# Sample attention of a hybrid decoder step as one list of steps over all its segments

## The chip, the cores and the metric

One NeuronCore of a Trainium2 chip runs the whole program in one launch. The metric is the device time of that launch in microseconds (us), as the median of several runs. Engines: PE is TensorE, ACT ScalarE, DVE VectorE, POOL GpSimd, SP SyncE (it only issues DMAs).

## What is computed

Two layers of a decoder, each with a convolution group and a sparse-attention group side by side. There are 512 prompt tokens and 8 sample tokens, one for each of 8 sequences that have 4096 past positions in a paged cache. For each sample token and each of 4 key heads the reference does:

```
s_c = q . k_cmp * scale            # 64 compressed blocks, softmax -> p_c, o_c
imp = sum of p_c over the 4 query heads of a key head
top 16 of 64 blocks by imp (first and last blocks forced)
s_s = q_rot . k_sel * scale        # 16 chosen blocks x 64 positions, softmax -> o_s
s_w = q_rot . k_win * scale        # last 512 positions, softmax -> o_w
o   = g0 * o_c + g1 * o_s + g2 * o_w
```

The chosen blocks differ by sequence and by head, so their keys and values (64 floats each) are fetched from the cache in HBM by indirect DMA. Beside this, in the same stage, the 520 tokens are multiplied by the columns of `w_in` that feed the convolution (values, gates), the attention gate `za` and the convolution gate `zc`; a 31-tap convolution, a layer norm and two gates follow.

## The kernel before

A tile framework orders each engine's instructions: program order gives the priority, and an instruction is placed once a simulated timeline holds it ready, so a lower-priority one can go ahead. `issue_after(mark)` forbids instructions of a block to be placed ahead of `mark` on the mark's engine. Each layer has four stages: `phase_a1` (first projections, and the compression of the cache), `phase_a2` (lines 815 to 1262, the stage of this change), `phase_b` (prompt attention) and `phase_c` (output product and next norm).

**The matrix product.** `gemm` (L322) works through jobs of 256 columns; a yield closes each chunk of four 128-row slices of weights (24 matmuls per half chunk, two halves), and one more closes the job. A 512 KB weight DMA (L332) fills `wf`; for each half, `split` (L373) makes a rounded part `wh` on ACT (L374) and the rest `wl` on DVE (L375), three buffers of each, at high priority; PE then runs three products (L350 to L352). `g.pe_mark` is the last matmul of the chunk (L357).

**The stage `phase_a2`.** `_interleave` (L136) mixes two generators, `proj2` with weight 80 and `sample` with weight RATE_S = 90: whichever has the fewer steps per weight goes next. `proj2` (L921) has 75 yields in the first layer and 80 in the second. `_behind` (L148) wraps `sample`: what it emits in a step is placed on PE behind the latest `g.pe_mark`. Ahead of both, L832 to L836 load the convolution weights, transpose them on PE (`pw`, L835) and copy them on DVE (`cwt`, L836).

**The generator `sample`** (L932). Its first step scores the compressed blocks, ranks them and makes the gather indices `six` (L1023). Then, for each half `rho` of the sequences, `comp_seg` and three calls of `segment` follow one another: the first half of the chosen blocks, the window, the second half. A segment covers four sequences. `keys_of` (L1068) fetches a tile of 128 positions with four indirect DMAs on POOL, one for each head (L1112, into `G2`, two buffers), copies keys (`kc`, L1122) and values (`vt`, L1131) on ACT, and transposes the keys on PE (`kpt`, L1126); a page of the newest positions comes with one more (L1097). All of a tile's work is emitted in one step:

```
for h in range(4):
    nc.gpsimd.indirect_dma_start(out=G[:np_, h, :], ...)
nc.scalar.activation(kc_..., G[:np_, :, 0:64], AF.Copy)
for hp in range(2):
    nc.tensor.transpose(pts[hp][:, j * 128:j * 128 + np_], kc_[...], ident[...])
nc.scalar.activation(vt_..., G[:np_, :, 256:320], AF.Copy)
if j < 3:
    yield None
```

There are three tiles per sequence in the first half and four in the second: 56 tiles and 224 gathers a layer besides the eight page rows. After a segment's last sequence, `segment` (L1148) runs its scores (`pss`, L1163), the maximum (`st_m`, L1176), the exponential (`ssc`, L1179), the transposes (`ptp_s`, L1190), the copy (`pts`, L1195 or L1198) and the products with the values (`pos_`, L1203) in one step; the sums into the output (`o_a`, `o_s`, L1038 and L1040) are a step of their own. The next segment's keys are emitted behind that. PSUM gives this generator three buffers (`mi`): two hold `kpt`, one `pss`. At the end L1249 transposes `o_s` (`pto`), and `phase_b` begins.

Of the kernel before, what the change touches and what calls it, by code (L numbers as in the profile page):

```python
# [10 lines left out]
F32 = mybir.dt.float32  # L11
# [18 lines left out]
SV = 5  # L30
# [3 lines left out]
RATE_S = 90  # L34
G2B = 2
# [286 lines left out]
def gemm(g, jobs, rhs, evac):  # L322
    nc, tc = g.nc, g.tc
    gps, wp = (g.gp, g.sp.gp2), g.wp
    for wsrc, c0, mi_, hs, (k0, k1), width in jobs:
# [3 lines left out]
        for kc in range(k0, k1, kf):  # L329
# [5 lines left out]
            for k2 in range(0, kf, kh):  # L335
# [479 lines left out]
def phase_a2(g, l, u):  # L815
# [5 lines left out]
    with ExitStack() as s2:  # L821
# [11 lines left out]
        pw = mi.tile([128, 512], F32, tag="mi", name="pw")  # L833
        for i in range(CT):
            nc.tensor.transpose(pw[:, i * CW:(i + 1) * CW], cwn[:, i * 128:(i + 1) * 128], ident[:CW, :CW])  # L835
        nc.vector.tensor_copy(cwt.rearrange("p a b -> p (a b)"), pw[:, :CT * CW])  # L836
# [8 lines left out]
        gst = {}  # L845

# [86 lines left out]
        def sample():  # L933
# [134 lines left out]
            def keys_of(rho, kind, half):  # L1068
                sps = (2 * rho, 2 * rho + 1)
                for s2 in range(2):  # L1070
                    for sp in sps:
                        s = 2 * sp + s2
                        kk = []
                        pts = [mi.tile([128, 512], F32, tag="mi", name="kpt") for _ in range(2)]
                        vt_ = pool.tile([128, 4, 256], F32, tag="sv", name="vt_", bufs=SV)
                        if kind == 1:
                            for part_ in range(2):
                                wt = vt_ if part_ else pool.tile([128, 4, 256], F32, tag="wk", name="wk")
                                nc.sync.dma_start(
                                    wt, a["cache_win"][l, s, :, part_].rearrange("(p j) h d -> p j (h d)", j=4)  # L1080
                                )
                                nc.sync.dma_start(
                                    wt[0:1, 0], kvs_d[s:s + 1, (4 + part_) * 256:(5 + part_) * 256]
                                )
                                if part_ == 0:
                                    for hp in range(2):
                                        for j in range(4):
                                            nc.tensor.transpose(
                                                pts[hp][:, j * 128:(j + 1) * 128],
                                                wt[:, j, hp * 128:(hp + 1) * 128],  # L1090
                                                ident,
                                            )
                        else:
                            for j in range(4):
                                if half == 0 and j == 0:
                                    G = pool.tile([128, 512], F32, tag="G0", name="G0", bufs=1)
                                    nc.gpsimd.indirect_dma_start(  # L1097
                                        out=G,
                                        out_offset=None,
                                        in_=g.rows,  # L1100
                                        in_offset=bass.IndirectOffsetOnAxis(ap=g.fix[:, s:s + 1], axis=0),
                                        element_offset=lrow * ROWF + 512,
                                    )
                                    for hp in range(2):
                                        nc.tensor.transpose(pts[hp][:, :128], G[:, hp * 128:(hp + 1) * 128], ident)
                                    nc.scalar.activation(vt_[:, 0], G[:, 256:512], AF.Copy)
                                    continue
                                jt = 4 * half + j - 1
                                np_ = 64 if jt == 6 else 128
                                G = pool.tile([128, 4, 320], F32, tag="G2", name="G2", bufs=G2B)  # L1110
                                for h in range(4):
                                    nc.gpsimd.indirect_dma_start(  # L1112
                                        out=G[:np_, h, :],
                                        out_offset=None,
                                        in_=g.pages64,
                                        in_offset=bass.IndirectOffsetOnAxis(
                                            ap=six[:np_, s * 4 + h, jt:jt + 1], axis=0
                                        ),
                                        element_offset=lrow * ROWF + 512 + h * 64,
                                    )  # L1120
                                kc_ = pool.tile([128, 256], F32, tag="kc", name="kc_", bufs=1)
                                nc.scalar.activation(  # L1122
                                    kc_[:np_].rearrange("p (h d) -> p h d", h=4), G[:np_, :, 0:64], AF.Copy
                                )
                                for hp in range(2):
                                    nc.tensor.transpose(  # L1126
                                        pts[hp][:, j * 128:j * 128 + np_],
                                        kc_[:np_, hp * 128:(hp + 1) * 128],
                                        ident[:np_, :np_],
                                    )  # L1130
                                nc.scalar.activation(  # L1131
                                    vt_[:np_, j].rearrange("p (h d) -> p h d", h=4), G[:np_, :, 256:320], AF.Copy
                                )
                                if j < 3:
                                    yield None
# [103 lines left out]
            for rho in range(2):  # L1239
                comp_seg(rho)  # L1240
                yield from segment(rho, 0, 0)
                while g.all_kv < l:
                    yield
# [428 lines left out]
```

## Time and profile before

| what | value |
|---|---|
| median of 3 runs | 3020.23 us (3012.37 to 3028.97) |
| profiled execution: time | 3029.22 us |
| profiled execution: span of its instructions | 3027.1 us |
| mean granted TensorE clock | 0.963 |
| PE, DVE, POOL, ACT busy | 90%, 75%, 57%, 48% of the span |
| HBM traffic | 182 GB/s over the span |

The profiled execution is one run of the program; its time is 2.1 us more than the span from its first to its last instruction. Times of rows count from the span's start. A busy PE includes stretches in which its clock was granted at half speed. The stage `phase_a2` runs from about 636 to 1131 us in the first layer and from about 2107 to 2619 us in the second; work of neighbouring stages overlaps its ends.

### The profile page before, as it was taken

Reading aid. Unit: us, or ns where it says so; the run is one execution under the profiler, and the core shown is the slowest. Engines: PE = TensorE matmul, PEld = TensorE weight load, DVE = VectorE, ACT = ScalarE, POOL = GpSimd, SP = SyncE. Lnnn points to the kernel's source line nnn. Section 1 sums busy time; section 2 is a strip of 40 time slices with the busy share of each in tenths; the row PEclk is TensorE's granted clock in tenths of the full one; section 3 lists DMA queues with packets and bytes.
Section 4 is the critical chain, followed back from the end, with each engine's and each line's share of the span. In section 5 each row is a group of like instructions: output and inputs, shape, how many; then the busy total and the mean of one; then the engine's idle time right before and its main releaser. Section 6 shows DMA issues by size and latency. Waiting matters only on the chain. (4 is left out here: it accounts for less than half of the span.)

```text
span 3027.1 us, 53793 instructions
## 1 busy us (share of the span) xinstructions
PE 2716.8 (90%) x18984; PEld 2378.5 (79%) x18984; DVE 2278.1 (75%) x4432; ACT 1446.6 (48%) x3180; POOL 1713.4 (57%) x1610
## 2 busy tenths in 40 slices
PE   7998989988989989888988899999998899998896
PEld 6787878777778778767877788887877778886795
DVE  7899988867877535885889978886687774379756
ACT  5444444433333545773556534444333345468644
POOL 4766676637466456764655735664556565467402
PEclk9999999999989999999999999999999999999998
DMA  8777777645455446316777766775555464563254
GB/s 264 228 210 213 210 210 236 194 119 186 151 160 174 132 148 199 118 36 188 213 237 217 236 208 202 208 228 144 161 181 151 128 214 146 153 186 97 61 161 155
DMA packets 430317, 534.48 MB, mean 177 GB/s; under 512 B 68450, under 2 KB 357362, under 8 KB 429760
## 3 DMA queue, kind: packets, MB, share of 16 engines
q1 hardware_dynamic: 367328, 324.42, 35.9%
q0 software_dynamic: 62720, 206.63, 22.2%
q8 instruction: 149, 2.44, 0.3%
q14 instruction: 120, 0.98, 0.1%
HBM read 484.80 MB, written 64.75 MB: 182 GB/s over the span
## 5 line engine op out<-in xcount | busy, mean ns | idle before, releaser
L350 PE MATMUL g<-uh,wh 128*128 128x256 f32 (+1 forms) x3328 | 962.5, 292 | 18.6 <-ACT wh L374 8.6
L351 PE MATMUL g<-ul,wh 128*128 128x256 f32 (+1 forms) x3328 | 958.9, 290 | 0.0
L352 PE MATMUL g<-uh,wl 128*128 128x256 f32 (+1 forms) x3328 | 944.2, 291 | 9.9 <-DVE wl L375 9.8
L539 POOL DMA_INDIRECT G<-in_cache_kv_pages_dram,gix x512 | 542.5, 1059 | 326.5 <-DVE T L550 161.0
L1112 POOL DMA_INDIRECT G<-in_cache_kv_pages_dram,six x448 | 494.8, 1104 | 336.7 <-issue 115.7
L375 DVE TENSOR_TENSOR wl<-wf,wh 128x512 fp32r<-128x512 f32 x565 | 427.7, 760 | 342.2 <-ACT wh L374 331.5
L350 PEld LDWEIGHTS g<-uh,wh 128*128 128x128 f32 x3328 | 643.9, 194 | 52.5 <-issue 13.9
L351 PEld LDWEIGHTS g<-ul,wh 128*128 128x128 f32 x3328 | 645.0, 194 | 23.2 <-issue 15.3
L352 PEld LDWEIGHTS g<-uh,wl 128*128 128x128 f32 x3328 | 635.3, 194 | 32.2 <-DVE wl L375 12.9
L374 ACT ACTIVATE wh<-wf 128x512 fp32r<-128x512 f32 x616 | 381.7, 625 | 417.4 <-PE g L351 275.2
L375 DVE TENSOR_TENSOR tl<-T,th 128x512 fp32r<-128x512 f32 x512 | 435.5, 869 | 90.4 <-ACT th L374 88.1
L374 ACT ACTIVATE th<-T 128x512 fp32r<-128x512 f32 x512 | 309.8, 624 | 315.9 <-DVE T L550 220.5
L550 DVE STREAM_TRANSPOSE T<-G 128x512 f32<-128x512 f32 x512 | 349.8, 695 | 24.9 <-DMA G<-in_cache_kv_pages_dram,gix 23.2
L887 DVE SCALAR_TENSOR_TENSOR c<-ap,cwt,c 128x512 f32<-128x512 f32 x480 | 339.9, 748 | 0.1
L579 PE MATMUL ca<-tl,w1h 128*128 128x512 f32 x512 | 217.9, 426 | 43.4 <-DVE tl L375 42.9
L375 POOL TENSOR_TENSOR w1l<-w1f,w1h 128x512 fp32r<-128x512 f32 x128 | 170.3, 1332 | 135.2 <-ACT w1h L374 99.4
L578 PE MATMUL ca<-th,w1h 128*128 128x512 f32 x512 | 215.8, 422 | 28.3 <-ACT th L374 17.6
L580 PE MATMUL ca<-th,w1l 128*128 128x512 f32 x512 | 209.5, 409 | 0.2 <-POOL w1l L375 0.2
L1376 POOL TENSOR_TENSOR smx<-smx,su 128x256 f32<-128x256 f32 (+2 forms) x192 | 153.8, 828 | 89.6 <-DVE su L1370 61.2
L1368 ACT ACTIVATE smx<-smx,nm 128x128 f32<-128x128 f32 (+3 forms) x256 | 140.8, 552 | 45.5 <-DVE nm L1364 43.0
L350 PE MATMUL g<-mha,wh 128*128 128x256 f32 (+1 forms) x512 | 146.7, 296 | 12.7 <-ACT wh L374 6.3
L374 ACT ACTIVATE w1h<-w1f 128x512 fp32r<-128x512 f32 x128 | 79.3, 623 | 158.8 <-DMA w1f<-in_cmp_w_dram 98.7
(1179 smaller groups left out, 5236.0 us busy)
## 6 DMA issues: line engine op xcount, KB each, us to landing
wf<-in_w_in_dram SPq DMA_DIRECT2D x220, 512.0 KB
wf<-in_w_out_dram SPq DMA_DIRECT2D x88, 512.0 KB
w1f<-in_cmp_w_dram SPq DMA_DIRECT2D x512, 64.0 KB
out_dram<-in_cache_win_dram SPq DMA_DIRECT2D x16, 1022.0 KB
G<-in_cache_kv_pages_dram,gix POOLq DMA_INDIRECT x512, 5.0
wk<-in_cache_win_dram SPq DMA_DIRECT2D x16, 512.0 KB
qq<-qr_d SPq DMA_DIRECT2D x64, 128.0 KB
G<-in_cache_kv_pages_dram,six POOLq DMA_INDIRECT x448, 3.2
```

The lines of the kernel that those rows point to most:

```text
L350: nc.tensor.matmul(ps[m][h], lh, xh[:, sl], start=first, stop=False)
L351: nc.tensor.matmul(ps[m][h], lh, xl[:, sl], start=False, stop=False)
L352: pe = nc.tensor.matmul(ps[m][h], ll, xh[:, sl], start=False, stop=last)
L374: g.nc.scalar.activation(dst_h, src, AF.Copy)
L375: return (eng or g.nc.vector).tensor_tensor(dst_l, src, dst_h.bitcast(F32), op=ALU.subtract)
L539: nc.gpsimd.indirect_dma_start(out=G[:, i, :], out_offset=None, in_=g.pages, in_offset=bass.IndirectOffsetOnAxis(ap=g.gix[:, un * 4 + hs:u ...
L550: nc.vector.transpose(T.rearrange("p a b c -> p a (b c)"), G[:, :, c * 256:(c + 1) * 256])
L578: nc.tensor.matmul(acc[c], w1h[:, c, e], hi, start=f, stop=False)
L579: nc.tensor.matmul(acc[c], w1h[:, c, e], lo, start=False, stop=False)
L580: nc.tensor.matmul(acc[c], w1l[:, c, e], hi, start=False, stop=la)
L887: ce.scalar_tensor_tensor(c[:, :SEQ], ap[:, j:j + SEQ], cwt[:, i, j:j + 1], c[:, :SEQ], op0=ALU.mult, op1=ALU.add)
L1112: nc.gpsimd.indirect_dma_start(out=G[:np_, h, :], out_offset=None, in_=g.pages64, in_offset=bass.IndirectOffsetOnAxis(ap=six[:np_, s * 4 + ...
```

## The change

`sample` becomes one list of steps over all six segments. Each step first does one pending softmax stage, if there is one, then issues the loads of its own tile, and then finishes (copies, transposes) the tile whose loads the step before issued. The scores, the transposes with the copy, and the value products of a segment are three entries of the pending list, so they fall into the steps that follow, beside the next segment's tiles; both `comp_seg` calls come first. What the sample emits on ACT is placed behind the latest `wh` split as well. The transposes of the convolution weights move behind the first job of `proj2`. RATE_S goes from 90 to 86. The number of buffers, DMAs, matmuls and copies stays as it was. The diff, cut to its core:

```diff
-RATE_S = 90
+RATE_S = 86
 def _behind(g, gen, on=True):
-    g.pe_mark = None
+    g.pe_mark = g.act_mark = None
...
-            for mark in (g.pe_mark if on else None, g.dve_mark):
+            for mark in (g.pe_mark if on else None, g.act_mark if on else None, g.dve_mark):
 # gemm
                     split(g, wh, wl, wf[:, k2:k2 + kh], weights_engine(g))
+                g.act_mark = g.last_act
 # split
-    g.nc.scalar.activation(dst_h, src, AF.Copy)
+    g.last_act = g.nc.scalar.activation(dst_h, src, AF.Copy).ins
 # phase_a2
-        pw = mi.tile([128, 512], F32, tag="mi", name="pw")
-        for i in range(CT):
-            nc.tensor.transpose(pw[...], cwn[...], ident[:CW, :CW])
-        nc.vector.tensor_copy(cwt..., pw[:, :CT * CW])
+        def conv_weights():      # the same five lines
...
                 yield from gemm(g, _jobs(w_in, C_A, [p]), u, ev_a)
+                if p == 0:
+                    conv_weights()
                 yield from gemm(g, _jobs(w_in, C_G, [p]), u, ev_g)
-            def keys_of(rho, kind, half):
-            def segment(rho, kind, half):
+            def load(q, at):          # the window's DMAs, or the gathers of one step
+            def finish(q, last, loaded):   # kc, vt, kpt; with the last tile ks_, then:
+                sg.vts[q.s] = q.vt
+                sg.pend.append(q)
+                if len(sg.pend) == 2:
+                    todo.append(lambda: scores(sg))
+                    if len(sg.vts) == 4:
+                        todo.extend((lambda: weigh(sg), lambda: values(sg)))
+            def scores(sg):   # pss; with the second pair st_m, nm, ssc
+            def weigh(sg):    # ptp_s, pts
+            def values(sg):   # pos_, then the sums into o_a or o_s
-            for rho in range(2):
-                comp_seg(rho)
-                yield from segment(rho, 0, 0)
-                ...
-                yield from segment(rho, 1, 0)
-                yield from segment(rho, 0, 1)
+            steps = []
+            for rho in range(2):
+                for kind, half in ((0, 0), (1, 0), (0, 1)):
+                    ...
+                    for n_ in range(4):
+                        js = ((0, 1), (2,), (3,)) if half == 0 else ((0,), (1,), (2,), (3,))
+                        ...
+                        if kind == 1:
+                            steps += [(q, 0, True)] + [None] * (2 if n_ == 0 else 1)
+                        else:
+                            steps += [(q, at, at == len(js) - 1) for at in range(len(js))]
+            todo = [lambda: comp_seg(0), lambda: comp_seg(1)]
+            prev = None
+            for step in steps + [None]:
+                if todo:
+                    todo.pop(0)()
+                new = None
+                if step is not None:
+                    ...
+                    new = (q, last, load(q, at))
+                if prev is not None:
+                    finish(*prev)
+                prev = new
+                yield
+            while todo:
+                todo.pop(0)()
+                yield
```

## Rows read from the trace of the kernel before

**Rows 1.** Stretches of the span, stage by stage (`phase_a1`, `phase_a2`, `phase_b` and `phase_c` with the next `phase_a1`, then the second layer): length, busy us (instructions) of each engine, granted PE clock, DMA share, GB/s.
```profile
core 0: us, PE busy (x) PEld busy (x) DVE busy (x) ACT busy (x) POOL busy (x), PEclk, DMA share, GB/s
0.00:636.00 636.00, 559.20 (x3755) 490.38 (x3755) 541.83 (x931) 286.75 (x528) 399.20 (x364) 0.97 0.72 214
636.00:1131.00 495.00, 447.60 (x3301) 387.54 (x3301) 333.20 (x610) 196.39 (x442) 283.85 (x257) 0.94 0.51 157
1131.00:1375.00 244.00, 221.50 (x1427) 186.18 (x1428) 177.37 (x531) 168.25 (x457) 156.54 (x162) 0.97 0.37 114
...
2107.00:2619.00 512.00, 471.00 (x3573) 416.03 (x3572) 342.50 (x630) 203.79 (x456) 290.72 (x260) 0.97 0.52 158
```

**Rows 2.** Waits of PE in the first layer's stage, 636 to 1131 us: total us, times, longest us. The `kpt` rows of L1126 are 18 (one for each wait, 29.7 us together); the first and the last of them stand here.
```profile
PE ptp_s L1190 <- ACT ssc L1179: 6.5, 2, 3.5
PE pw L835 <- DMA chp<-in_conv_b_dram: 4.2, 1, 4.2
...
PE kpt L1126 <- ACT kc__10080 L1122: 3.6, 1, 3.6
...
PE kpt L1126 <- ACT kc__9646 L1122: 0.2, 1, 0.2
```

**Rows 3.** The same of the second layer's stage, 2107 to 2619 us; the `kpt` rows are 17 (25.8 us together), first and last shown.
```profile
PE pw L835 <- DMA chp<-in_conv_ln_g_dram: 5.1, 1, 5.1
PE ptp_s L1190 <- ACT ssc L1179: 5.0, 1, 5.0
PE kpt L1126 <- ACT kc__24642 L1122: 4.1, 1, 4.1
...
PE kpt L1126 <- ACT kc__24962 L1122: 0.2, 1, 0.2
```

**Rows 4.** Timeline of one tile in the first segment: its first and its last gather, the copy of its keys, the transposes. Start us, us, instruction, idle time of the engine before it and what ended it.
```profile
711.79 0.96 POOL L1112 DMA_INDIRECT G<-in_cache_kv_pages_dram,six  x1 [0.30 <-issue]
...
715.63 1.09 POOL L1112 DMA_INDIRECT G<-in_cache_kv_pages_dram,six  x1 [0.30 <-issue]
...
721.38 0.42 ACT L1122 ACTIVATE kc__7744<-G 128x256 f32<-128x256 f32 x1 [6.21 <-DMA G<-in_cache_kv_pages_dram,six]
...
721.85 0.44 PE L1126 MATMUL kpt<-const,kc__7744 128*128 128x128 f32 x2 [3.21 <-ACT kc__7744 L1122]
```

**Rows 5.** Timeline of another tile: its first gather and the copy of its keys.
```profile
872.34 1.01 POOL L1112 DMA_INDIRECT G<-in_cache_kv_pages_dram,six  x1 [0.30 <-issue]
...
879.62 0.42 ACT L1122 ACTIVATE kc__9646<-G 64x256 f32<-64x256 f32 x1 [3.77 <-DMA G<-in_cache_kv_pages_dram,six]
```

**Rows 6.** The gathers of L1112 in 636 to 1131 us: ns min/median/max of one, first and last start; and what ended POOL's idle time before them (us, times).
```profile
L1112 POOL DMA_INDIRECT G<-in_cache_kv_pages_dram,six x224: 893/962/2971, 662.6 to 1108.6; - x112
...
  issue: 57.4, 190
```

**Rows 7.** Timeline of PE at the end of one segment: last scores, transposes of the exponentials, first value product, first transposes of the next segment's keys.
```profile
991.74 1.04 PE L1163 MATMUL pss<-ks__10621,qz_r 128*32 128x512 f32 x2
...
997.35 0.46 PE L1190 MATMUL ptp_s<-const,ssc 64*128 64x64 f32 x4
...
1000.88 0.40 PE L1203 MATMUL pos__10701<-vt__9849,pts 128*32 128x256 f32 x1
...
1004.46 0.77 PE L1088 MATMUL kpt<-const,wk 128*128 128x128 f32 x5
```

**Rows 8.** Waits of POOL in 636 to 1131 us: total us, times, longest us.
```profile
POOL G L1112 <- ACT kc__11343 L1122: 19.2, 1, 19.2
POOL G L1097 <- PE kpt L1126: 15.6, 1, 15.6
POOL G L1112 <- ACT vt__11269 L1131: 11.8, 1, 11.8
```

**Rows 9.** Short stretches, with the columns of Rows 1: three in which PE stood still for a part (two of them with the stretch right after), and one of full work.
```profile
718.00:724.00 6.00, 2.79 (x24) 2.59 (x23) 1.90 (x4) 1.88 (x5) 4.48 (x6) 1.00 0.91 311
...
897.00:908.00 11.00, 7.67 (x40) 4.15 (x40) 5.54 (x12) 3.89 (x9) 2.04 (x4) 0.53 0.25 89
908.00:919.00 11.00, 11.00 (x92) 9.85 (x89) 10.75 (x23) 3.70 (x11) 1.31 (x1) 1.00 0.18 51
...
2160.00:2167.00 7.00, 2.91 (x25) 2.69 (x25) 3.85 (x7) 1.00 (x3) 5.63 (x5) 1.00 0.60 169
2167.00:2171.00 4.00, 4.00 (x23) 4.00 (x22) 3.72 (x7) 2.70 (x7) 3.24 (x3) 0.57 0.67 196
2475.00:2550.00 75.00, 75.00 (x576) 63.77 (x575) 39.58 (x72) 43.82 (x84) 33.99 (x30) 1.00 0.48 148
```

**Rows 10.** Timeline of PE at the end of the first layer's stage: the last tile's transposes, the last segment's transposes of exponentials, the transpose of the output.
```profile
1115.46 0.47 PE L1126 MATMUL kpt<-const,kc__12097 64*128 64x64 f32 x2
...
1122.54 0.60 PE L1190 MATMUL ptp_s<-const,ssc 64*128 64x64 f32 x4 [3.00 <-ACT ssc L1179]
...
1131.25 0.27 PE L1249 MATMUL pto<-const,o_s 128*64 128x128 f32 x1 [2.79 <-DVE o_s L1040]
```

**Rows 11.** Waits of ACT in 636 to 1131 us, the longest entry.
```profile
ACT wh L374 <- PE g L351: 85.9, 58, 4.4
```

**Rows 12.** Timeline of DVE at the start of the first layer's stage: the copy of the convolution weights and the gather indices.
```profile
637.92 0.42 DVE L836 COPY cwt<-pw 128x248 f32<-128x248 f32 x1 [7.74 <-PE pw L835]
...
661.88 0.48 DVE L1023 TENSOR_SCALAR six<-pix,const 128x256 int32<-128x256 f32 x1
```

More of the change, by code (lines that the diff above doesn't have):

```diff
@@ L845, in phase_a2 @@
         gst = {}
+        def conv_weights():
+            pw = mi.tile([128, 512], F32, tag="mi", name="pw")
+            for i in range(CT):
+                nc.tensor.transpose(pw[:, i * CW:(i + 1) * CW], cwn[:, i * 128:(i + 1) * 128], ident[:CW, :CW])
+            nc.vector.tensor_copy(cwt.rearrange("p a b -> p (a b)"), pw[:, :CT * CW])
         def ev_a(i, ps):
@@ L1066, in comp_seg @@
                 gather(g.o_s, po, rows, K["hm4"], True)
-            def keys_of(rho, kind, half):
[L1069 to L1135, printed above, removed]
-                            if half == 1:
-                                nc.sync.dma_start(vt_[64:65, 3], kvs_d[s:s + 1, 3 * 256:4 * 256])
-                        tail_ = kind == 0 and half == 1
-                        for hp in range(2):
-                            ks_ = pool.tile([128, 512], F32, tag="ks", name="ks_", bufs=4)
-                            w0 = 448 if tail_ else 512
-                            nc.scalar.activation(ks_[:, :w0], pts[hp][:, :w0], AF.Copy)
-                            if tail_:
-                                nc.scalar.activation(ks_[:, 448:449], g.kts[:, 0, hp, s:s + 1], AF.Copy)
-                            kk.append(ks_)
-                        yield s, s2, sp, kk, vt_
@@ L1148, in segment @@
-            def segment(rho, kind, half):
-                rows = slice(64 * rho, 64 * rho + 64)
-                sps = (2 * rho, 2 * rho + 1)
-                tail_ = kind == 0 and half == 1
-                width = 449 if tail_ else 512
-                pss = mi.tile([128, 512], F32, tag="mi", name="pss")
-                vts, pend = {}, []
-                for v in keys_of(rho, kind, half):
-                    if v is not None:
-                        s, s2, sp, kk, vt_ = v
-                        vts[s] = vt_
-                        pend.append((s2, sp, kk))
-                    if len(pend) == 2:
-                        for hp in range(2):
-                            for s2, sp, kk in pend:
-                                nc.tensor.matmul(
-                                    pss[32 * sp:32 * sp + 32, :width],
-                                    g.qz_r[:, hp, sp, s2 * 32:(s2 + 1) * 32],
-                                    kk[hp][:, :width],
-                                    start=(s2 == 0 and hp == 0),
-                                    stop=(s2 == 1 and hp == 1),
-                                    tile_position=(0, 32 * sp),
-                                )
-                        pend = []
-                    yield
-                col = half if kind == 0 else 0
-                m_, l_ = (st_m, st_l) if kind == 0 else (st_t[:, 0:1], st_t[:, 1:2])
@@ new lines, in scores @@
+            def scores(sg):
+                if sg.pss is None:
+                    sg.pss = mi.tile([128, 512], F32, tag="mi", name="pss")
+                for hp in range(2):
+                    for q in sg.pend:
+                        nc.tensor.matmul(
+                            sg.pss[32 * q.sp:32 * q.sp + 32, :sg.width],
+                            g.qz_r[:, hp, q.sp, q.s2 * 32:(q.s2 + 1) * 32],
+                            q.kk[hp][:, :sg.width],
+                            start=(q.s2 == 0 and hp == 0),
+                            stop=(q.s2 == 1 and hp == 1),
+                            tile_position=(0, 32 * q.sp),
+                        )
+                sg.pend.clear()
+                if len(sg.vts) < 4:
+                    return
+                rows, pss, width = sg.rows, sg.pss, sg.width
+                sg.pss = None
+                col = sg.half if sg.kind == 0 else 0
+                m_, l_ = (st_m, st_l) if sg.kind == 0 else (st_t[:, 0:1], st_t[:, 1:2])
@@ L1217, in segment @@
                     gather(g.o_s, po, rows, hmf, False)
-                elif half == 0:
+                elif sg.half == 0:
                     gather(o_a, po, rows, K["hm"], True)
```

116 lines of the change are left out of this document (101 added, 15 removed).

## The prediction

> **What bounds the kernel now.** I read the stretches by stage first [rows 1]: PE is the fullest engine in every stage, and in the two `phase_a2` stages, which are all that the change touches, it is busy for 447.6 of 495 us and 471.0 of 512 us. So 47.4 and 41.0 us, 88.4 together, are idle time of the bounding engine. The other loss stands in the clock column: 0.94 and 0.97 granted, so 0.06 x 495 + 0.03 x 512 = 45.1 us of clock are lost. DVE (333 and 343 us) and POOL (284 and 291) have room.
>
> Then the waits of PE [rows 2, 3]: most of its idle time ends with a `kc` copy, 29.7 us in 18 waits and 25.8 us in 17, so 55.5 us. Next come `ptp_s` behind the exponential (6.5 and 5.0) and `pw` behind a DMA (4.2 and 5.1). Waits for weights are not among the long rows, and ACT itself stood 85.9 us waiting for PE to give weight buffers back [rows 11]: weights come early enough.
>
> A single tile shows why [rows 4]. Its four gathers start at 711.79 to 715.63 us and the copy runs at 721.38, after ACT stood 6.2 us for the landing; the transposes follow at 721.85, and PE had stood 3.2 us. From first gather to copy it took 9.6 us here and 7.3 us in a quieter place [rows 5]. PE's instructions run in order, so the transposes, put where the schedule thought the tile would be there, hold all matmuls behind them. The buffers are not what delays the gathers: 190 of 224 had no wait but POOL's own 0.30 us of issue [rows 6], so a tile costs POOL 4 x (0.962 + 0.302) = 5.06 us.
>
> The list itself also stops. At one segment's end PE goes from the last scores at 991.74 over `ptp_s` (997.35) and `pos` (1000.88) to the next segment's keys at 1004.46 [rows 7]: 13 us without a tile, in which the two gather buffers are full. POOL then waits 19.2, 15.6 and 11.8 us [rows 8]. So the list runs behind its share, its instructions have the older priority, and the schedule puts transposes in as soon as it holds a tile ready.
>
> **The change, part by part.** Tiles consumed a step later: nothing is added or removed, only moved. `proj2` has 75 and 80 yields, so at 86 to 80 there are 80.6 and 86 steps; the first stage's PE work gives 447.6 / 80.6 = 5.55 us a step. The gathers of tile n wait for the buffer that the copies of tile n-2 free, so two steps, 11.1 us, must hold 0.8 us of copies and 7.3 to 9.6 us of gathering [rows 4, 5]. They do, with 0.7 to 3.0 us to spare, and the mark puts the transposes a chunk (5 to 6 us) later than today: more than the longest `kpt` wait of 4.1 us [rows 3]. But the list starts late: its indices are there at 661.88 us [rows 12], 26 us into the stage, so for the first segment (12 of the 56 tiles) it will be behind, and the placement as now. I leave 12/56 of 55.5, 11.9 us, and take **43.6 us**. POOL's queue gets the same gathers in the same order; the window's DMAs on SP's queue go a step earlier, their number unchanged.
>
> Softmax stages on steps of their own: each finds its input a step old. The `ptp_s` waits go, except the last segment of the first layer, where 3.0 us stood with nothing left to cover it [rows 10]: 6.5 + 5.0 - 3.0 = **8.5 us**. If the matmuls that should cover them are used up, this comes back as at the end.
>
> `pw` moved behind the first job of `proj2`: between 0 (the schedule may still put it ahead of its DMA's landing) and 9.3 us [rows 2, 3]. It is freed of priority over the stage's first matmuls but not of the DMA, so I take half, **4.6 us**. The 7.7 us that DVE stood for it [rows 12] then go to the ranking, which only brings the list in earlier.
>
> The clock: low stretches follow PE's pauses. After 2.91 busy us of 7, the granted clock of the next 4 us was 0.57; in 897 to 908 with 7.67 of 11 it was 0.53, and back at 1.00 in the next 11 us of full work [rows 9]. These are the half level, 1.2 GHz, and the full one. I remove 43.6 + 8.5 + 4.6 = 56.7 of 88.4 idle us, 64%, and take the same part of 45.1: **28.9 us**. Bounds: 0, and 45.1.
>
> The mark on ACT: the sample's copies now stand behind a weight split. That costs nothing while PE still has the chunk to run; if that cover is gone, matmuls wait for `wh`. The rate of 86 lets the list end at 79 of 80.6 steps in the first layer, where it had 77 of 84.4: nominally later, but the list now keeps its place, and ended at 1131 us only because it ran behind [rows 10]. I count nothing for it.
>
> What is late next: no row shows the new waits. Between 0 (a stretch of 75 us ran with PE at 75.00 and clock 1.00 [rows 9]) and 30 us (2.5 us, half of the longer `ptp_s` wait, at each of 12 segments); I take 12 us, 1 us each, nearer to the full stretch since the pending stages have a step each.
>
> There is one more price to weigh. The gathers took 962 ns at the median and 893 at the least while DVE was busy for 333 of 495 us [rows 1, 6], so a denser DVE adds nothing. The Trainium skill (SBUF — State Buffer, Who interferes with whom) says that a DVE instruction with two SBUF inputs blocks a GpSimd instruction that reads SBUF. By that rule, with every gather at the longest of the row, 2971 ns, a tile would take 13.1 us of POOL and nothing would be gained; the median speaks against it.
>
> Sum: 43.6 + 8.5 + 4.6 + 28.9 - 12 = 73.6 us off the profiled 3029.2, which makes 2955.6. That run lies 9 us above the median of 3020.2 and inside the runs' spread; off the median it is **2947 us**. The range of this case goes from 2910 (all `kpt`, `ptp_s` but the last, and `pw` gone: 73.3 us, with 83% of the clock, 37.4) to 2995 (half of the `kpt` waits, no `pw`, 42% of the clock, 30 us of new waits).
>
> **The rivals.** First: the two gather buffers bind. They stay two; if a tile's gathers cannot start before the tile two ahead is copied, and that copy comes a step later too, the distance has not grown, and PE waits as before. For it: POOL did stand for copies at segment ends [rows 8]. Against it: the 190 gathers that waited for issue alone [rows 6]. Then 8.5 + 4.6 us remain: 3007 us. The Trainium skill (Perfetto Trace Analysis, Optimization Strategy) states a rule like it: a gap that repeats on the engine that should be full can mean that there is no buffer for the next tile. By that rule the order would not matter.
>
> Second, slower: the copies at ACT's head. They now wait for the split of the latest chunk, and ACT waits 85.9 / 58 = 1.5 us for PE before such a split [rows 11]. Past the 0.7 to 3.0 us to spare, buffers come free a step late: a pair of tiles takes 9.6 + 0.8 + 5.55 = 16.0 us, 56 tiles take 447, and with 26 us at the start, 18 window steps (100) and 15.8 at the end [rows 10, 12] the list needs 589 us: 94 and 77 more than the stages have now. With half of that covered by matmuls brought forward, 3020 + 85 = 3105 us.
>
> Third: it does not quite do what it says. With its four page rows a first-half tile costs POOL 13 x 1.264 / 3 = 5.48 us, hardly less than a step of 5.55, and less idle time makes the step shorter. Then the list falls behind in the gather segments, and the schedule places transposes early again. Half of `kpt` and clock stay: 73.6 - 36.2 = 37 us, 2983 us.
>
> **How the numbers follow.** The forecast gets 0.72, as each term stands on a wait of its own row; the buffers 0.12, the slower one 0.08, the third 0.08. Half a percent, 15 us, is about what a measurement of this kernel tells from no change. Faster is the forecast and the third, 0.80; the same is the buffers, 0.12; slower is 0.08. The range goes from 2905 to 3010: it takes in the forecast's range, the third and the buffers, and leaves out the slower case.
>
> **What would show it.** Right: in both stages PE's waits for `kc` fall from 55.5 to some 12 us, nearly all in the first segment; `ptp_s` keeps one short wait; the stages' clock reads 0.97 to 0.99; next-segment `kpt` rows lie between a segment's `pss` and `pos`; POOL has no wait of over 10 us at segment ends except in the window. Wrong: `kpt` waits as long as before with POOL waiting for copies (buffers), waits of PE for `wh` behind a `kc` that stands for its gather (ACT), or a first-layer stage whose end lies past 1131 us.

## The result, and the profile after

The changed kernel takes 3053.0 us (median, 3048.6 to 3062.4) against 3019.4 us of the kernel before: a ratio of 1.0113, interval 1.0075 to 1.0152. It is slower by 1.1%, where the prediction said 2.4% faster. Run twice more, it gave 1.0107 (1.0071 to 1.0143) and 1.0115 (1.0085 to 1.0145). The profiled execution has a span of 3047.7 us at a mean clock of 0.956; that of before 3027.1 us at 0.963.

Kernels measured side by side form a group, and every ratio is to the kernel before of the same group; in three of the groups below, named groups with gaps, the kernel before took some 3143 us and not 3018, and TensorE's rows show gaps that no releaser ended.

The two `phase_a2` stages of the changed kernel, and the stretch of each in which PE stood still longest (the columns of Rows 1):

```profile
core 0: us, PE busy (x) PEld busy (x) DVE busy (x) ACT busy (x) POOL busy (x), PEclk, DMA share, GB/s
627.00:1135.00 508.00, 437.62 (x3282) 382.80 (x3281) 328.08 (x610) 198.78 (x440) 290.40 (x259) 0.94 0.50 151
2109.00:2636.00 527.00, 468.50 (x3538) 414.77 (x3537) 345.12 (x629) 207.23 (x456) 284.92 (x254) 0.94 0.50 153
1050.00:1081.00 31.00, 5.42 (x18) 3.95 (x19) 12.31 (x18) 12.64 (x20) 13.49 (x13) 0.51 0.16 44
2559.00:2587.00 28.00, 8.18 (x32) 6.20 (x33) 13.00 (x19) 13.16 (x23) 8.35 (x8) 0.51 0.16 48
```

The stages were to get shorter; they are 508 and 527 us against 495 and 512 [rows 1]. PE is idle for 70.4 and 58.5 us of them, against 47.4 and 41.0. Of this, 25.6 and 19.8 us lie in the two short stretches of the last rows, near the end of each stage, where the granted clock was 0.51. The first stage ends at 1135 us, past the 1131 us that the prediction had set as a sign of being wrong.

PE's waits in the first layer's stage (total us, times, longest); the rows for `kc` are 15, together 39.7 us, first and last shown:

```profile
PE p_sum L388 <- POOL lacc L912: 16.6, 1, 16.6
PE g L351 <- DVE zc L461: 9.0, 1, 9.0
PE kpt L1138 <- ACT kc__10344 L1131: 7.6, 1, 7.6
...
PE kpt L1138 <- ACT kc__8159 L1131: 0.2, 1, 0.2
```

And in the second layer's; 17 rows for `kc`, together 33.8 us:

```profile
PE g L351 <- DVE zc L461: 10.6, 2, 9.0
PE kpt L1138 <- ACT kc__29492 L1131: 6.3, 1, 6.3
...
PE p_sum L388 <- POOL lacc L912: 4.0, 1, 4.0
...
PE ptp_s L1201 <- ACT ssc L1187: 1.6, 1, 1.6
```

Beside [rows 2, 3]: `pw` is gone, `ptp_s` has 1.6 us left of 11.5, both as predicted. The waits for `kc` have not fallen to 12 us; they are 39.7 + 33.8 = 73.5 us where they were 55.5. At the top stand two rows that the prediction did not have: `p_sum` for GpSimd, and `g` for `zc`. Both belong to the convolution's layer norm (`ln_stats`). POOL's timeline there, start us first:

```profile
1037.37 1.17 POOL L1101 DMA_INDIRECT G<-in_cache_kv_pages_dram,six  x1 [0.30 <-issue]
1038.56 1.31 POOL L912 TENSOR_TENSOR lacc<-lacc,csq 128x520 f32<-128x520 f32 x1
...
1044.98 1.30 POOL L912 TENSOR_TENSOR lacc<-lacc,csq 128x520 f32<-128x520 f32 x1
1046.44 0.96 POOL L1101 DMA_INDIRECT G<-in_cache_kv_pages_dram,six  x1 [0.16 <-issue]
...
1051.18 1.29 POOL L912 TENSOR_TENSOR lacc<-lacc,csq 128x520 f32<-128x520 f32 x1
...
1063.35 2.64 POOL L912 TENSOR_TENSOR lacc<-lacc,csq 128x520 f32<-128x520 f32 x2
```

The seven additions of squares now stand among the last segment's gathers, four gathers to an addition, 6.0 to 6.7 us apart (the last two follow each other): 34 us for all seven. In the kernel before they took 12 us, in the window segment. The two rows, after first (ns min/median/max of one, first and last start):

```profile
L912 POOL TENSOR_TENSOR lacc<-lacc,csq x7: 1277/1289/1316, 1031.8 to 1064.7; 128x520 f32<-128x520 f32 x7
```
```profile
L909 POOL TENSOR_TENSOR lacc<-lacc,csq x7: 1303/1317/1643, 1012.3 to 1022.5; 128x520 f32<-128x520 f32 x7
```

There they were inside a stretch in which POOL had no gather that it could start (its next one, after 19.2 us of waiting for a buffer, is in [rows 8]). The layer norm is where it was in `proj2`; the list has moved past it. PE, in order, meets the sum next:

```profile
1048.98 0.44 PE L1138 MATMUL kpt<-const,kc__11970 128*128 128x128 f32 x2 [3.48 <-ACT kc__11970 L1131]
1066.05 1.22 PE L388 MATMUL p_sum<-lacc,ones 128*128 128x256 f32 x2 [16.62 <-POOL lacc L912]
1067.83 1.25 PE L388 MATMUL p_sum<-lacc,ones 128*128 128x264 f32 x2 [0.56 <-ACT lacc L380]
1078.05 0.58 PE L351 MATMUL g<-uh,wh 128*128 128x256 f32 x1 [8.97 <-DVE zc L461]
```

The second wait follows from the first: what hangs on the late sum stands on DVE ahead of the evacuation `zc` that gives PE its accumulators back.

```profile
1067.81 3.62 DVE L381 RECIPROCAL lacc<-lacc 128x256 f32<-128x256 f32 x2 [23.03 <-ACT lacc L380]
1071.47 4.97 DVE L921 TENSOR_TENSOR c<-c,lacc 128x520 f32<-128x520 f32 x8
...
1077.58 1.43 DVE L461 TENSOR_TENSOR zc<-g,rms 128x256 f32<-128x256 f32 x4
```

### The profile page after: what moved, and what is told of

Read it like the earlier page. It is cut to its first block, busy times and chain, and to the rows that moved or that the text cites. A ratio compares the mean times of both kernels' runs of the same rounds, so it can differ in the third digit from the quotient of the medians.

```text
span 3047.7 us, 53784 instructions
## 1 busy us (share of the span) xinstructions
PE 2709.3 (89%) x18984; PEld 2378.2 (78%) x18984; DVE 2261.1 (74%) x4432; ACT 1458.6 (48%) x3190; POOL 1723.8 (57%) x1610
## 5 line engine op out<-in xcount | busy, mean ns | idle before, releaser
L351 PE MATMUL g<-uh,wh 128*128 128x256 f32 (+1 forms) x3328 | 966.5, 293 | 38.2 <-DVE zc L461 19.6
L1101 POOL DMA_INDIRECT G<-in_cache_kv_pages_dram,six x448 | 513.2, 1146 | 361.3 <-issue 108.9
L351 PEld LDWEIGHTS g<-uh,wh 128*128 128x128 f32 x3328 | 644.5, 194 | 68.8 <-DVE zc L461 21.3
L376 DVE TENSOR_TENSOR tl<-T,th 128x512 fp32r<-128x512 f32 x512 | 421.6, 844 | 100.1 <-ACT th L375 97.8
L890 DVE SCALAR_TENSOR_TENSOR c<-ap,cwt,c 128x512 f32<-128x512 f32 x480 | 342.8, 752 | 0.6
L351 PE MATMUL g<-mha,wh 128*128 128x264 f32 (+1 forms) x512 | 145.5, 292 | 14.7 <-DVE zg L1554 8.8
```

What stands on the lines that cost most here:

```text
L351: nc.tensor.matmul(ps[m][h], lh, xh[:, sl], start=first, stop=False)
L890: ce.scalar_tensor_tensor(c[:, :SEQ], ap[:, j:j + SEQ], cwt[:, i, j:j + 1], c[:, :SEQ], op0=ALU.mult, op1=ALU.add)
L1101: nc.gpsimd.indirect_dma_start(out=G[:np_, h, :], out_offset=None, in_=g.pages64, in_offset=bass.IndirectOffsetOnAxis(ap=six[:np_, s * 4 + ...
```

## Experiments

**The layer norm's additions off GpSimd**, in both kernels (L912 of the changed one, L909 of before):

```diff
-                    nc.gpsimd.tensor_tensor(acc, acc, sq, op=ALU.add)
+                    nc.vector.tensor_tensor(acc, acc, sq, op=ALU.add)
```

> The changed kernel with one edit: the layer norm's seven additions of squares per layer (L912) run on VectorE instead of GpSimd. Theory A (the layer norm's sums now meet the last gathers in GpSimd's queue, one addition per four gathers, and TensorE stands behind them): the waits of p_sum for GpSimd (16.6 us in layer 0, 4.0 in layer 1) go, the low clock behind them (30.7 and 27.3 us at half clock) goes in part, time 2995 to 3025. Theory B (the loss is in the gather waits, which are as many as before and longer singly: 39.5 and 33.9 us; the layer norm only moves a wait that would appear at the next tile): 3040 to 3060.

> The kernel before with the same edit (additions of squares on VectorE). Theory A: no gathers stand in GpSimd's queue at the layer norm there, so nothing to win: within 0.4% of the kernel before, 3008 to 3032. Theory B has the same number; a gain like that of the changed kernel's would say that the additions cost GpSimd's time anywhere, and that the change did not bring the collision.

In this group (one with gaps, kernel before 3141.7 us) the changed kernel with the edit came to 0.9909 of it (0.9876 to 0.9941), the kernel before with the edit to 0.9938 (0.9915 to 0.9961). The first is theory A's direction; the second missed its number (0.6% where 0.4% was the limit), and the changed kernel itself was not in the group. So the set was run again side by side, with the kernel before at 3017.9 us:

> The changed kernel as it is, as the partner of the next two. On a chip where TensorE has no gaps without a releaser (kernel before about 3017 us): 1.007 to 1.015 of the kernel before. On a chip with such gaps (kernel before about 3143 us), where the nearly equal kernel without the third mark came out at 0.9996: 0.995 to 1.005.

> The changed kernel with the layer norm's additions on VectorE. If the collision with the layer norm is the cause of the loss: 0.8 to 2.0% below the changed kernel of this call, and within 0.6% of the kernel before with the same edit. If the rest of the order is: within 0.5% of the changed kernel, and 0.7 to 1.5% above the kernel before with the same edit.

> The kernel before with the layer norm's additions on VectorE: by the first run of this edit 0.994 of the kernel before. If that was the additions' place in GpSimd's queue ahead of the gathers behind them, again 0.990 to 0.998, on any chip; if it belongs to that chip, 0.998 to 1.004 on one without the gaps.

Measured: the changed kernel 3047.5 us, 1.0115 (1.0085 to 1.0145); with the edit 3006.7 us, 0.9971 (0.9950 to 0.9991); the kernel before with the edit 3019.4 us, 1.0019 (0.9997 to 1.0040). So the edit takes 40.8 us (1.3%) from the changed kernel and nothing from the kernel before (1.5 us more, inside the interval): the collision is brought by the change, and it is more than the whole loss. With both on VectorE the changed kernel is 12.7 us faster, and in the group with gaps 13.1 us (3112.0 against 3125.1). That the edit won 0.6% from the kernel before in that group and nothing here stays open. The changed kernel with the edit beats both kernels; it was run twice more, in groups with gaps:

> The changed kernel with the layer norm's additions on VectorE, again, for a chip on which TensorE has no gaps without a releaser. Theory A: the ratio to the kernel before falls from 1.011 by 0.8 to 2.0%, to 0.991 to 1.003; the wait of p_sum for GpSimd (17.0 and 4.1 us) is gone, and the half clock of the two stages is 40 to 70 us instead of 85 and 55. Theory B (gather waits only): 1.005 to 1.013.

> The changed kernel with the layer norm's additions on VectorE, as the partner of the other run: 0.994 to 1.000 of the kernel before where TensorE has no gaps without a releaser, 0.988 to 0.996 where it has them.

It came to 0.9919 (0.9881 to 0.9956) and 0.9899 (0.9862 to 0.9936). In the run at 3006.7 us, its additions and its two stages:

```profile
L912 DVE TENSOR_TENSOR lacc<-lacc,csq x7: 687/694/701, 1026.6 to 1034.2; 128x520 f32<-128x520 f32 x7
```
```profile
624.00:1110.00 486.00, 440.05 (x3289) 386.06 (x3285) 332.22 (x617) 198.93 (x440) 279.43 (x252) 0.95 0.50 158
2091.00:2592.00 501.00, 465.28 (x3544) 411.06 (x3543) 344.98 (x637) 206.98 (x456) 277.20 (x247) 0.98 0.51 161
```

All seven additions are done in 8.3 us, no `p_sum` wait for them is left, and `g` for `zc` keeps 6.8 us. What is left is `kc`: 34.2 us in the first layer and 25.4 in the second, 59.6 together. The kernel before with the same edit, in the same group, has 31.4 and 28.4, 59.8 together; the changed kernel without it 68.6. So some 9 us of these waits went with the layer norm's edit, and beyond the collision the change leaves the waits for `kc` as they were. That is theory B's part.

**The step of delay undone** (each tile consumed in the step of its gathers; everything else stays):

```diff
                     new = (q, last, load(q, at))
-                if prev is not None:
-                    finish(*prev)
-                prev = new
+                    finish(*new)
```

> The changed kernel as it is, on the chip of this call, as the partner of the other three. If this chip has the same balance as the first: ratio to the kernel before 1.007 to 1.015. If it behaves like the chip of the four runs above, where the kernel without the third mark (only a few places in TensorE's and ScalarE's order differ) came out at 0.9996: 0.997 to 1.003.

> The kernel before as it is, for a profile on the chip of this call. The waits for kc should be as on the first chip, 29.7 and 25.8 us. On the chip of the four runs above, TensorE stood 65 to 85 us in gaps that no releaser ended; if this chip does that too, it is the chip's and not a variant's.

> The changed kernel with each tile consumed in the step of its own gathers; the one list, the spread softmax stages, the marks and the moved weights' transposes stay. My prediction gave the delay 43.6 of the 55.5 us of waits for kc, so by it the waits would be 15 to 20 us longer in each layer than the changed kernel's 39.5 and 33.9. If the list is planned behind its gathers anyway (it starts 8 to 9 steps late), the step of room never exists and the delay is worth nothing: the same waits within 8 us and the same time within 0.6%.

Measured side by side: 1.0107 (1.0071 to 1.0143) with the delay, 1.0140 (1.0104 to 1.0176) without. The intervals overlap, and the waits of `p_sum` for GpSimd differ too (10.5 and 1.5 us without the delay, 17.0 and 4.1 with it), so the waits for `kc` say more than the times: 38.6 and 39.9 us without it and 39.1 and 31.2 with it; the kernel before, in the same group, has 30.2 and 19.6 us and no gaps without a releaser. The delay is worth 0 to 9 us of waits, not 15 to 20 in each layer.

The traces show why. From a tile's first gather to its transposes it takes 9.6 us without the delay and 9.8 us with it (medians of the 112 tiles of a run, same group), and 9.5 us in the kernel before. The edit moved the step in the program, but hardly the place of the transposes behind their gathers.

**The late list.** I first held that the delay had no room because the list starts 8 to 9 product steps late. Nine empty steps ahead of the first gather, and a faster list so that it still ends in time:

```diff
-RATE_S = 86
+RATE_S = 98
...
+            for _ in range(9):
+                yield
             todo = [lambda: comp_seg(0), lambda: comp_seg(1)]
```

> The changed kernel with nine empty steps behind the index step and RATE_S 98 for 86, so that the list is planned no earlier than it can run. Theory C (the list runs some 9 steps late from its first gather on, because the index step takes 20 us; transposes are then put as early as the plan holds them ready, and the one step of room is never given): the kc waits of the transposes fall from 39.5 and 33.9 us to under 15 in each layer, and the layer norm's collision stays or grows, 3010 to 3045. Rival D (a gather of 0.9 to 5.7 us is longer than the room of one step, however it is planned): kc waits stay at 30 or more in each layer, 3045 to 3075.

> The changed kernel with both edits: nine empty steps behind the index step with RATE_S 98, and the layer norm's additions on VectorE. If the two causes (a late list, and the collision with the layer norm) are separate, the gains add: each alone came out at 0.991 and 0.992 of the kernel before, together 0.980 to 0.986. If they are the same time seen twice (both pull the gathers and the layer norm apart): 0.988 to 0.993.

Alone: 0.9924 (0.9894 to 0.9954) of 3141.7 us, with `kc` waits of 26.3 and 11.5 us, and 6.5 and 12.7 us more that no releaser ended. With the layer norm's edit, in a group without such gaps: 1.0000 (0.9977 to 1.0023), `kc` waits 42.4 and 31.1 us. These are not shorter than the changed kernel's, though the first tile was now only 2 steps late. This theory falls. The shift itself eased the collision: without the layer norm's edit, `p_sum` waits for GpSimd 4.2 us in the first layer and not at all in the second.

**Another pace** (the layer norm's edit, and RATE_S 82):

> The changed kernel with the layer norm's additions on VectorE and a slower list, RATE_S 82 for 86 (a step every 0.98 of a product step instead of 0.93, about 6.0 us against GpSimd's 6.0 us for a tile). Theory P: the transposes stand as far apart as the gathers need, once the late start is made up; waits for kc under 25 and 20 us, and 0.985 to 0.995 of the kernel before, unless the list's end then sticks out behind the products (up to 10 us in each layer). If the pace does not matter: the same as the layer norm's edit alone, within 0.4%.

> The changed kernel with the layer norm's additions on VectorE and RATE_S 82 for 86, again. If the plan's spacing against GpSimd's 6.0 us for a tile makes the waits: waits for kc of 15 to 25 us in layer 0 and 12 to 20 in layer 1 (34 and 25 with RATE_S 86), 0.987 to 0.995 of the kernel before. If the spacing is not what the rate sets (the late list is planned without regard to it): the same as with RATE_S 86, 0.994 to 1.000.

The first run gave 0.9897 (0.9843 to 0.9952), beside 0.9919 for RATE_S 86 in the same group; the second 0.9949 (0.9928 to 0.9971) beside 0.9899. The waits for `kc` were 27.0 and 23.5 us, then 13.2 and 26.7, beside 14.0 and 19.5, then 17.3 and 18.6. No gain in either; both groups have gaps, and the slower list was not run in one without.

**The mark on ACT left out:**

```diff
-            for mark in (g.pe_mark if on else None, g.act_mark if on else None, g.dve_mark):
+            for mark in (g.pe_mark if on else None, g.dve_mark):
```

> The changed kernel without the third mark (a list step no longer waits in the plan for ScalarE's last split of weights). If the mark holds ScalarE's copies back (my rival of before): kc waits shorter, 3010 to 3040. If it binds nowhere, because the list is behind its marks nearly always: 3045 to 3060. If it keeps ScalarE's copies out of the way of the weights' splits: waits of g for wh appear (more than the 0 and 3.8 us of now), 3060 to 3080.

0.9996 (0.9977 to 1.0015) in the first group, one with gaps; the changed kernel itself was not in it, so the time decides little. The `p_sum` wait is 16.6 us here too. In the orders of PE, ACT and DVE only a few instructions change place (25 of 18984, 46 of 3190 and 6 of 4432), and none on POOL and SP: the mark binds almost nowhere, and my rival on it had no ground.

**Half of the gathers** (heads 2 and 3 of a tile take the rows of heads 0 and 1; copies and transposes keep their number and size), with the delay, without it, and in the kernel before:

```diff
-                    for h in range(4):
+                    for h in range(2):
                         nc.gpsimd.indirect_dma_start(
                             out=G[:np_, h, :],
...
-  kc_[:np_].rearrange("p (h d) -> p h d", h=4), G[:np_, :, 0:64]
+  kc_[:np_].rearrange("p (x h d) -> p x h d", x=2, h=2), G[:np_, None, 0:2, 0:64].to_broadcast([np_, 2, 2, 64])
```

> The changed kernel with two gathers for a tile instead of four: heads 2 and 3 of a tile are left out and take the rows of heads 0 and 1; copies, transposes and all later work keep their number and size. Theory P (GpSimd's own pace makes the waits: gathers run without a break, 6.0 us for a tile, while the transposes stand 5.0 to 5.7 us apart in TensorE's order, so no earlier start helps): the tile's period falls to about 3 us and the waits for kc from 39 and 31 us to under 10 in each layer; the layer norm's wait shrinks to about half (17 to 9 us); time 2960 to 3000 on a chip where the changed kernel takes 3047. Rival L (the waits are the landing of the last gather and the copy behind it, some 3.5 us, in the step after): waits stay above 20 us in each layer, time 3010 to 3040.

> The same two gathers for a tile (heads 2 and 3 left out as before), and each tile consumed in the step of its own gathers. Under theory P the step of delay can work only where the gathers do not set the pace: here it should be worth what I gave it, 10 to 40 us (waits for kc of 10 to 25 us in each layer against under 10 with the delay). If the delay is worth nothing even so: within 0.4% of the kernel with two gathers and the delay.

> The kernel before with two gathers for a tile instead of four (heads 2 and 3 left out, as in the changed kernel's run). If GpSimd's pace made the waits there too: waits for kc under 15 us in each layer. The changed kernel with two gathers came to 2976 us. If the change is worth its spread softmax stages and moved transposes once the gathers are out of the way (13 us by my prediction's terms), this one comes to 2980 to 2995; if its order costs the same here as with four gathers, to 2940 to 2970.

With the delay 2976.2 us, 0.9439 (0.9398 to 0.9481); without it 2967.5 us, 0.9408 (0.9364 to 0.9451), both in a group with gaps, the kernel before at 3145.2. The kernel before with half came to 2956.9 us, 0.9805 (0.9773 to 0.9838), in the group with 3017.9; the ratios of the two groups are not to be compared. The waits for `kc` shrink to 12.0 and 3.4 us, 8.4 and 2.2 us, and 9.1 and 7.2 us. The stages of the first of them:

```profile
627.00:1097.00 470.00, 428.76 (x3316) 377.34 (x3315) 330.86 (x611) 200.36 (x445) 172.75 (x147) 0.97 0.41 127
2060.00:2563.00 503.00, 485.43 (x3793) 434.37 (x3790) 361.10 (x664) 226.13 (x490) 179.34 (x156) 0.98 0.43 133
```

The clean pair is the kernel before: 9.1 and 7.2 us with half of the gathers, 31.4 and 28.4 with all of them (and the layer norm's edit) in the same group. For the changed kernel the partner of its group, the one with the layer norm's edit, has 14.0 and 19.5 us. So the waits hang on the amount of gathering, in either kernel, and the delay is worth nothing even where gathers do not fill GpSimd. Half of the gathers shortens two things at once, POOL's time for a tile and the time from a tile's first gather to its last; which of the two makes the waits is not separated.

## Why the prediction was wrong, point by point

**The `kpt` term (43.6 us), and with it the clock's 28.9.** The step that failed is "the mark puts the transposes a chunk later than today: more than the longest `kpt` wait". They do not stand a chunk (5 to 6 us) later: from a tile's first gather to its transposes the median is 10.2 us in this profile and 9.7 in that of before, and undoing the delay took 0.2 us from it. The waits rose by 18.0 us. The rows had said that gathering itself has no slack, and I read them for another end: 190 of 224 gathers waited for nothing but issue [rows 6]. I took that to mean that the buffers leave room. It also means that POOL hardly stops in a gather segment, so that a later step in the program does not bring one gather earlier. In the changed kernel it is the same (183 of 224):

```profile
L1101 POOL DMA_INDIRECT G<-in_cache_kv_pages_dram,six x224: 897/951/5310, 652.4 to 1102.6; - x112
...
  issue: 54.8, 183
```

I priced a tile by the median, 5.06 us, and 5.48 with the page rows. In the first segment of each layer the changed kernel's 12 tiles took 68.8 and 71.3 us of POOL, 5.7 and 5.9 us each, and in the fourth (the next half's first gathers) 87.5 and 81.3, 7.3 and 6.8 each; the step was to be 5.55. The longest wait, 7.6 us for `kc__10344`, stands behind two gathers far above the median:

```profile
892.15 4.01 POOL L1101 DMA_INDIRECT G<-in_cache_kv_pages_dram,six  x1 [0.30 <-issue]
896.47 4.78 POOL L1101 DMA_INDIRECT G<-in_cache_kv_pages_dram,six  x1 [0.30 <-issue]
901.56 0.94 POOL L1101 DMA_INDIRECT G<-in_cache_kv_pages_dram,six  x1 [0.30 <-issue]
902.81 0.95 POOL L1101 DMA_INDIRECT G<-in_cache_kv_pages_dram,six  x1 [0.31 <-issue]
```

This tile took 11.6 us of POOL, where I had 5.06. Such gathers were there before: the row that I read was the first layer's, with 2.97 us at most [rows 6], and the second layer's has 7.77:

```profile
L1112 POOL DMA_INDIRECT G<-in_cache_kv_pages_dram,six x224: 893/958/7774, 2143.5 to 2592.8; - x112
```

So "the median speaks against it" was the wrong test. In the two profiles all gathers of over 2 us, 11 of 448 before and 13 of 448 after, ran beside the convolution's instruction on DVE, whose two tensors `ap` and `c` lie in SBUF (L887 of before, L890 of after), with DVE busy for 70 to 100% of the gather. DVE through the first of the two gathers above, in part:

```profile
892.35 0.74 DVE L890 SCALAR_TENSOR_TENSOR c<-ap,cwt,c 128x512 f32<-128x512 f32 x1
...
893.34 0.68 DVE L376 TENSOR_TENSOR wl<-wf,wh 128x512 fp32r<-128x512 f32 x1
893.94 1.41 DVE L890 SCALAR_TENSOR_TENSOR c<-ap,cwt,c 128x512 f32<-128x512 f32 x2
```

Gathers with that instruction beside them took 1.21 us on average before and 1.31 after; those without took 0.97 and 0.98, and none of them more than 1.69. This fits the rule weighed in the prediction (the Trainium skill, SBUF — State Buffer, Who interferes with whom: VectorE's two-input instructions hold up GpSimd's reads). It is not shown as a cause, as no run took VectorE's work away from beside the gathers. My third rival, with POOL's pace against the step, had the right place for these waits, but gave half of the gain back where all of it went; and a slower list, which by it should have helped, did not in the two groups where it ran.

**What was not in the sum: the layer norm.** I wrote "POOL's queue gets the same gathers in the same order", and looked at no other work of that queue. Counted by the products ahead of its transposes in PE's order, the list of the first layer ran some 10 steps late before; in the changed kernel it is 9 steps late at the first tile and 1 or less in the last segment. The layer norm had fallen into a window segment by that lateness. Made less late, the gathers meet the additions. Price by the edit: 40.8 us. By rows, and not all of it the collision's: 25.6 and 19.8 us of PE's idle time in the two stretches, and 13.6 us of work at half clock. This alone turns the sign. The chance of 0.08 for slower stood on ACT's mark, so that the kernel came out slower bears out none of that rival. The range had taken up to 30 us of new waits, but spread over the segments' ends.

**`ptp_s` (8.5) and `pw` (4.6).** Right, and sized low: of 20.8 us of such waits [rows 2, 3] 1.6 are left, so 9.9 and 9.3 us are gone. The 12.7 us by which the changed kernel leads, both with the edit, are near the terms' sum, 13.1, and that is in part luck: in that pair 16.6 us of these waits are gone, and those for `zc` are 6.0 us longer (7.3 against 1.3). One term by itself was not run.

**The clock.** Not gained: the stages' clock is 0.94 and 0.94 against 0.94 and 0.97 [rows 1], and the half level sits where PE stood (0.51 in both stretches). With the edit the first layer's stage reads 0.95 and the second's 0.98, in the kernel before with the edit 0.97 and 0.96. The clock fell where PE stood, as the prediction had it; the waits did not go.

**New waits at segment ends (12).** Sized too high: among PE's rows the longest wait for a segment's softmax stages is the 1.6 us of `ptp_s`.

**A term outside the stage.** At the start of `phase_c` PE waits 8.6 us for `zg` where it waited 3.1:

```profile
PE g L351 <- DVE zg L1554: 8.6, 1, 8.6
```
```profile
PE g L350 <- DVE zg L1514: 3.1, 1, 3.1
```

On SP's queue one weight load now goes ahead of the strided loads of the norm weights, where two did; the kernel with the layer norm's edit waits as long (8.4 us). But the kernel before with that edit waits 7.4 us, with the same order on the queue, and with half of the gathers 8.1. So this wait comes and goes with small shifts of order and is not a price of the change alone. I had counted only the two `phase_a2` stages.

**The rivals.** Buffers: by the rows not it, though no run had a third one. POOL's waits of over 10 us for copies stand at the third and fourth tile behind a window, as before; the one elsewhere, 21.2 us near the end of the first layer's stage, is 7.6 us with the layer norm's edit, so most of it is the late sum passed on. ACT's mark: nothing.

What stays open is what would shorten the waits for `kc` at the full amount of gathering, and whether the long gathers beside DVE's work make a part of them.

## What to carry to other kernels

An engine that issues without a pause can be the bound in that stretch, whatever its busy share over the stage (POOL: 57%). Here moving the consumer did not help, and fewer instructions on that engine did. Before a stream is moved, list everything else that is issued on its queues at the place where it will land, and ask who waits in order for that: here seven additions of 1.3 us cost 40.8. Where one generator's lateness has kept two streams apart, making it punctual is a change to both. And whether a step in the program has moved an instruction is read from the trace: here the place of the transposes behind their gathers had hardly changed.

## What the runs showed of the hardware

An indirect gather of up to 128 rows of 1280 bytes held POOL for 0.95 to 0.97 us at the median, and single ones beside VectorE's two-input work for 2 to 7.77 us. An addition of 128x520 took 1.29 us on POOL and 0.69 us on DVE.

In the groups with gaps, every profile of a kernel with all its gathers has gaps of PE that no releaser ended, 68 to 90 us in all, most of them (49 to 67 us) in the `phase_a2` stages. The kernel without the ACT mark shows them, with the changed kernel's stream for comparison in the second fence (busy us, mean ns, idle us before and what ended it):

```profile
L351 PE MATMUL g<-uh,wh 128*128 128x256 f32 (+1 forms) x3328 | 976.0, 295 | 49.6 <-DVE zc L461 17.9 <-issue 16.0 <-ACT wh L375 5.6
L352 PE MATMUL g<-ul,wh 128*128 128x256 f32 (+1 forms) x3328 | 968.7, 293 | 10.7 <-issue 10.6
```
```profile
L352 PE MATMUL g<-ul,wh 128*128 128x256 f32 (+1 forms) x3328 | 960.4, 290 | 0.0
```

With half of `phase_a2`'s gathers, in such a group, the same line lost 0.7 us in all, and the two stages 0 to 2.3 us; the 23 and 29 us of gaps elsewhere stayed. So in these stages the gaps came with the gathers' load; why some groups have them and others not is open. The same kernel, with the layer norm's edit, was thus worth 0.997 of the kernel before without gaps and 0.990 to 0.992 with them.
